# Low parts of the queries stored between zeros, so that products over 64 rows become products over 128, with an 8 KB descriptor scratch

## The chip, the cores and the metric

The kernel runs on one core of a Trainium2 chip. The time is device microseconds of one execution of the whole program, from inputs in HBM to the output in HBM; the figure for the kernel before is the median of three runs. TensorE (PE) does the matrix products, and its weight loads (PEld) are profiled beside them. VectorE (DVE), ScalarE (ACT) and GpSimd (POOL) do the elementwise work, SyncE (SP) issues most of the DMAs, POOL the others.

## The reference, cut to what matters

A trunk of four pre-norm residual layers over 512 tokens of width 1024. Layers 0 and 3 use differential attention (8 heads, two softmax maps each), layer 1 stick-breaking attention (16 heads), layer 2 sliding-window attention (16 query heads, 4 key heads). In all of them a query and a key have 64 channels, so that a score is a product over 64 channels:

```python
s = jnp.einsum('bqhjd,bkhjd->bhjqk', qb, k).astype(jnp.float32) * scale + bias   # layers 0, 3
z = jnp.einsum('bqhd,bkhd->bhqk', qb, k).astype(jnp.float32) * scale              # layer 1
s = jnp.einsum('bnqgrd,bnkgd->bngrqk', q, kb).astype(jnp.float32) * (SW_DIM ** -0.5) + bias  # layer 2
```

Each layer ends with a gated feed-forward block: an up projection to twice 2752 channels, a causal convolution of width 3, SiLU gate times value, and a down projection from 2752 channels, which are 21 blocks of 128 and a rest of 64.

## The kernel before

The residual lies with channels on the partitions, in eight chunks of 128 x 512. A product of float32 operands is made of three products of their high and low parts (`mm3`): high times high, high times low, low times high, summed in one bank of PSUM. The weights come in pieces of four 128 x 128 blocks through four raw tiles; ACT makes the high part, DVE the low part, each into a ring of four tiles. SP issues the weight loads in the order of use.

All work is written as tasks, and a planner emits each instruction in the order of its estimate of the engines' clocks. The result is one fixed queue per engine; an engine that waits holds up what stands behind it. The planner charges a product of n columns n / 2.4 ns (107 at least), whatever its number of rows, and 600 ns for a DMA on SP. It knows nothing of memsets, which are emitted when a layer's tiles are made.

**Queries and keys.** `to_qk` takes a projected chunk of 128 channels, which holds two heads or maps of 64 channels (its halves). DVE scales it out of PSUM into `qk_t`, ACT copies it to `hi`, POOL subtracts to make the low part, and four DMAs on SP stack the parts for each half: a query's high part twice (`qs`, 128 rows), a key's high and low part (`ks`, 128 rows). One product over 128 rows then gives two of the three terms. The third, a query's low part times a key's high part, is a product over the 64 rows of that half, read directly from the tile in which POOL put the low part (`ql`, ring of two, given back when the query's scores are done). The low parts of keys have a ring of one.

**Scores.** In layers 0, 2 and 3 `scores` makes both halves in four products: two over 128 rows (L665), then the two over 64 rows, one in the upper and one in the lower rows (L668). Layer 1 has the keys as weights, and alternates one product over 128 rows (L943) with one over 64 (L944).

**Down projection.** Each output chunk is 63 products over 128 rows and a tail for the last 64 channels: `gt_hl` has their high part in the upper and their low part in the lower 64 rows, `wt_hi` the weights' high part twice (L1341, 128 rows), `wt_lo` the weights' low part once (L1342, 64 rows). The last chunk of the last layer is made in two halves of 256 tokens.

Of the kernel before, what the change touches and what calls it, by code (L numbers as in the profile page):

```python
# [12 lines left out]
F32R = mybir.dt.float32r  # L13
# [22 lines left out]
# blocks of 128 rows per weight piece: inputs of width D, and of the down projection  # L36
KD = (4, 4)
KF = (4, 4, 4, 3, 3, 3)
# the very first pieces, for the first row block and for the others
FIRST = [(0, 1), (1, 4)], [(0, 4)]  # L40
# order of the output projection's (output chunk, head chunk) blocks: what needs the last heads comes late
# [23 lines left out]
# The work is written as tasks, generators that yield what they need next: an engine for an operation of some  # L65
# nanoseconds, which they emit when resumed; a tile of a ring; an event; or a delay. Everything is emitted in the
# order of an estimate of the engines' clocks, so that no engine's queue stands still for what another has yet to do.
# [33 lines left out]
class Ring:  # L101
    """Tiles in turn. Some users leave a few spare for those that must not starve."""
# [44 lines left out]
class Clock:  # L147
# [58 lines left out]
    def run(self, tasks):  # L206
        """Emit until these tasks are through."""
        while True:
            while self.todo:
                task, value = self.todo.popleft()  # L210
                self.t = task.t
                self.resume(task, value)
            if all(t.end.at is not None for t in tasks):
                return
            self.pick()
# [3 lines left out]
def trunk(ctx: ExitStack, tc: tile.TileContext, A, out):  # L219
# [60 lines left out]
    # the last product of all comes in halves of the tokens  # L280
# [48 lines left out]
    def rstd(ms, r, scale, cols=slice(0, T)):  # L329
        """r <- 1 / sqrt(scale * ms + EPS), the approximate root refined by a Newton step; ms is a bank, given back."""  # L330
        n = cols.stop - cols.start
        ms_, r = ms[:, :n], r[:, cols]
        lt = yield tmps
        ln = lt[:, :n]
        yield act(n, -2)
        nc.scalar.activation(ln, ms_, AF.Ln, scale=scale, bias=eps)
        vt = yield tmps
        v = vt[:, :n]
        yield dve(n, prio=-2)
        nc.vector.tensor_scalar(v, ms_, scale, EPS, ALU.mult, ALU.add)  # L340
        banks.give(ms)
        yield act(n, -2)
        nc.scalar.activation(r, ln, AF.Exp, scale=-0.5)
        tmps.give(lt)
        yield dve(n, 3, -2)
        nc.vector.scalar_tensor_tensor(v, v, -0.5, r, ALU.mult, ALU.mult)
        nc.vector.tensor_tensor(v, v, r, ALU.mult)
        nc.vector.scalar_tensor_tensor(r, v, 1.5, r, ALU.add, ALU.mult)
        tmps.give(vt)

    class Norm:
        """Takes the residual chunk by chunk; the gain goes in at once, the reciprocal root is applied later."""
# [68 lines left out]
    class LastNorm(Norm):  # L421
        """The last chunk comes in halves of the tokens, so that the first half's way out is hidden."""
# [79 lines left out]
    def product(pieces, parts, last=True, cols=slice(0, T)):  # L502
        """One product; returns its bank."""
        t = cols.stop - cols.start
        ps = yield banks
        k, K = 0, sum(pieces)
        for n in pieces:
            w = yield w_next()
            wh, wl = w_view(w)
            for j in range(n):  # L510
                xh, xl = yield parts[k]
                yield mm(t, t, t, prio=5)
                mm3(ps[:, :t], wh[:, j, :], wl[:, j, :], xh[:, cols], xl[:, cols], k == 0, last and k == K - 1)
                k += 1
            w_done(w)
        return ps

    def split_psum(ps, hi, lo, n=T):
        """A bank into two rings' tiles; gives the bank back."""
        h = yield hi  # L520
        yield act(n)
        copy(h[:, :n], ps[:, :n], AF.Copy)
        l = yield lo
        yield dve(n)
        nc.vector.tensor_tensor(l[:, :n], ps[:, :n], f(h[:, :n]), ALU.subtract)
        banks.give(ps)
        return h, l

    class Forms:
        """What an attention's projections become."""  # L530

        def __init__(self, pool, norm, l, v_bufs=3):
            self.norm, self.l = norm, l
            self.qk_t = ring(pool, "qk_t", 1)
            self.hi = ring(pool, "hi", 1, dtype=F32R)
            self.lo = {"q": ring(pool, "ql", 2, dtype=F32R), "k": ring(pool, "kl", 1, dtype=F32R)}
            self.st = {n: ring(pool, n + "s", 2, (P, 2, T), F32R) for n in "qk"}
            self.vh = ring(pool, "vh", v_bufs, dtype=F32R)
            self.vl = ring(pool, "vl", v_bufs, dtype=F32R)

        def values(self, got):
            """Two units' values, tokens on the partitions."""
# [20 lines left out]
        def to_v(self, ps, got):  # L563
            """Split [tokens of a block, (block, channels)] per unit."""
# [22 lines left out]
        def to_qk(self, ps, got, name, flip=False, lo_dve=False):  # L587
            """Split, and stacked for the products of 64 rows to take two terms at once. Per half of the channels:
            a query's high part twice, a key's high and low part. flip reverses the tokens within each block, as
            the bands of the biases want them."""  # L590
# [14 lines left out]
            lo = yield self.lo[name]  # L605
# [6 lines left out]
            for dst, src in ((st[top, 0], hi[top]), (st[bot, 1], hi[bot]), (st[bot, 0], other[top]), (st[top, 1], other[bot])):  # L612
                yield dma(-1)
                nc.sync.dma_start(out=f(dst), in_=f(src))
            clock.t += DMA_LAT
            self.hi.give(hi)
            if name == "k":
                self.lo[name].give(lo)
            got.set((st, lo))

        def q_done(self, q):
            self.st["q"].give(q[0])
            self.lo["q"].give(q[1])
# [4 lines left out]
        def first(self, us, flip):  # L628
            """The first two units' queries and keys, row block by row block as the residual arrives."""
# [17 lines left out]
        def qkv(self, us, flip):  # L647
            """All units' projections."""
# [12 lines left out]
    def scores(dst, q, k, qs, ks):  # L661
        """Both halves' products; those of 64 rows side by side, in the array's two halves."""
        (q2, ql), (k2, _) = q, k
        for half in range(2):
            nc.tensor.matmul(dst[half], q2[:, half, qs], k2[:, half, ks], start=True, stop=False)  # L665
        for half in range(2):
            rows = slice(64 * half, 64 * half + 64)
            nc.tensor.matmul(dst[half], ql[rows, qs], k2[rows, half, ks], start=False, stop=True)  # L668

# [73 lines left out]
    # per key block: which of three tiles its weights are in, and from which column  # L743
# [151 lines left out]
    def stick_attention(pool, norm, l, oh, ol, done, last_bank):  # L895
# [35 lines left out]
        def logit_steps():  # L931
            for i, hd in enumerate(heads):
# [3 lines left out]
                rows = slice(64 * half, 64 * half + 64)  # L936
                for kb in reversed(range(NB)):
# [6 lines left out]
                    nc.tensor.matmul(zb[:, :n], k2[rows, half, ks], ql[rows, kb * P:], start=False, stop=True)  # L944
# [24 lines left out]
        def weight_steps():  # L969
            for hd in heads:  # L970
                b = yield banks.spare(1)
                last = None
                for kb in reversed(range(NB)):
# [5 lines left out]
                    if last:  # L979
                        # the later block's sums, from those behind a key to those over the whole block  # L980
# [44 lines left out]
    def window_attention(pool, norm, l, oh, ol, done, last_bank):  # L1025
# [113 lines left out]
        def turn_steps(ats):  # L1139
            """Each half's weights turned, key blocks 0 and 1 into one tile, 2 and 3 into another."""  # L1140
# [14 lines left out]
        def value_steps(ats):  # L1155
            """Both halves at once, of which a half of the rows counts each. The banks have two query blocks each."""
# [65 lines left out]
    def feed_forward(pool, l, norm, nxt):  # L1222
# [8 lines left out]
        # the last 64 rows of the down projection, twice, to take both parts of g at once  # L1231
        wt_hi = pool.tile([P, D], F32R, name="wt_hi")
        wt_lo = pool.tile([P, D], F32R, name="wt_lo")
        g = [event() for _ in range(NFF)]
# [70 lines left out]
        def steps():  # L1305
            e = None
            # the first two side by side, while the last of the residual is on its way
# [24 lines left out]
            for m in range(ND):  # L1332
                ms = slice(m * P, m * P + P)
                halves = l == DEPTH - 1 and m == ND - 1
                for cols in (slice(0, T // 2), slice(T // 2, T)) if halves else (slice(0, T),):
# [6 lines left out]
                    nc.tensor.matmul(ps[:, :n], wt_lo[0:64, ms], gt_hl[0:64, cols], start=False, stop=True)  # L1342
# [49 lines left out]
def kmajor(w):  # L1392
    """[K, M] -> [M/128, 128 of K, K/128, 128 of M]"""
# [4 lines left out]
def layout(inp):  # L1398
    """Data layout only."""
# [5 lines left out]
    for l, w in enumerate(wq):  # L1405
        # queries and keys in chunks of 128 channels, values in groups of 256
# [8 lines left out]
    # the first two heads' queries and keys, all four chunks for a block of rows at a time  # L1415
# [20 lines left out]
    # constants of the shapes  # L1436
# [30 lines left out]
```

## Time and profile before

| | |
|---|---|
| median of three runs | 2419.07 us (2418.07 to 2422.58) |
| profiled execution: span from first to last instruction | 2418.2 us |
| PE / PEld busy | 2387.7 / 1939.6 us |
| DVE / ACT / POOL busy | 1620.8 / 1227.9 / 375.5 us |
| matrix products | 11271 |
| HBM read, mean rate over the span | 212.15 MB, 89 GB/s |

The span is that of the one execution that was profiled; its own time outside the profiler's span is not recorded, and the median of the three unprofiled runs lies 0.9 us above the span. A product's duration in the profile includes the time in the pipeline, so durations of neighbours overlap; distances between starts tell how fast PE takes them. In a row of PE, 64*128 means 64 rows of the array by 128 columns of weights, and 64x512 that 512 columns are moved through it.

### The profile page before, as it was taken

To read this page: it belongs to the slowest core of one execution; us is meant where nothing else is said; L and a number is where in the kernel's file an instruction comes from. 1 tells how busy PE (TensorE), PEld (TensorE's weight loads), DVE (VectorE), ACT (ScalarE), POOL (GpSimd) and SP (SyncE) were. 2 spreads that over 40 slices of the span, in tenths; PEclk is the share of its full clock that TensorE was granted. 3 is DMA by queue.
4 is the path that set the end of the run, shared out by engine and by line. 5 is a ranking of instruction groups with operands and counts; after the bars stand their busy time and mean duration, and the time that the engine had idled before them with its cause. 6 is when DMAs were issued, how large, how long until landed. Compare 5 with 4: busy or idle time off the path is not lost.

```text
span 2418.2 us, 32917 instructions
## 1 busy us (share of the span) xinstructions
PE 2387.7 (99%) x11271; PEld 1939.6 (80%) x11271; DVE 1620.8 (67%) x3054; ACT 1227.9 (51%) x2413; POOL 375.5 (16%) x385
## 2 busy tenths in 40 slices
PE   8999999999999999999999999999999999999998
PEld 6888788877877787888778888888778887888876
DVE  6886877733598878777335858776336876877624
ACT  4675544433476656444335855454334665544433
POOL 3442200000143322000001320000012433000001
PEclk9999999999999999999999999999999999999999
DMA  6442323233322223333334423333334442333333
GB/s 191 142 135 88 96 97 108 94 89 92 115 79 79 83 63 98 97 105 94 89 93 133 109 74 105 97 105 92 90 110 129 138 127 70 105 100 105 93 88 104
DMA packets 139031, 247.93 MB, mean 103 GB/s; under 512 B 17487, under 2 KB 32495, under 8 KB 138864
## 3 DMA queue, kind: packets, MB, share of 16 engines
q1 hardware_dynamic: 134736, 233.18, 31.7%
q0 software_dynamic: 4128, 12.66, 1.9%
q8 instruction: 88, 1.44, 0.2%
q14 instruction: 79, 0.65, 0.1%
HBM read 212.15 MB, written 2.16 MB: 89 GB/s over the span
## 4 chain that ended last, share of the span: by engine, by line
PE 62%; DVE 3%; ACT 1%; issue 1%; DMA 1%; POOL 0%; SPq 0%; DVEq 0%; ACTq 0%; POOLq 0%
PE ps L498 19%; PE ps L499 18%; PE ps L500 18%; PE ps L556 2%; PE ps L668 1%; DVE h_lo L366 1%; PE ps L665 1%; PE ps L1151 1%; DVE w_lo L291 1%; PE ps L1342 0%; PE ps L870 0%; PE ps L944 0%; DVE x L1197 0%; DMA ks<-kl 0%; PE ps L1341 0%
## 5 line engine op out<-in xcount | busy, mean ns | idle before, releaser
L288 ACT ACTIVATE w_hi<-w_raw 128x512 fp32r<-128x512 f32 (+2 forms) x775 | 477.5, 617 | 844.5 <-PE ps L499 691.8
L291 DVE TENSOR_TENSOR w_lo<-w_raw,w_hi 128x512 fp32r<-128x512 f32 (+2 forms) x775 | 535.0, 692 | 431.0 <-ACT w_hi L288 423.6
L498 PE MATMUL ps<-h_hi,w_hi 128*128 128x512 f32 x1840 | 728.6, 396 | 5.6 <-ACT h_hi L364 5.6
L499 PE MATMUL ps<-h_lo,w_hi 128*128 128x512 f32 x1840 | 721.5, 392 | 0.7
L500 PE MATMUL ps<-h_hi,w_lo 128*128 128x512 f32 x1840 | 719.4, 391 | 2.5 <-DVE w_lo L291 2.5
L498 PEld LDWEIGHTS ps<-h_hi,w_hi 128*128 128x128 f32 x1840 | 346.9, 189 | 84.6 <-ACT h_hi L364 5.6
L499 PEld LDWEIGHTS ps<-h_lo,w_hi 128*128 128x128 f32 x1840 | 347.1, 189 | 77.1 <-DVE h_lo L366 9.3
L500 PEld LDWEIGHTS ps<-h_hi,w_lo 128*128 128x128 f32 x1840 | 346.9, 189 | 75.6 <-DVE w_lo L291 2.9
L498 PE MATMUL ps<-gh,w_hi 128*128 128x512 f32 (+1 forms) x693 | 272.4, 393 | 0.0
L499 PE MATMUL ps<-gl,w_hi 128*128 128x512 f32 (+1 forms) x693 | 269.2, 388 | 0.0
L500 PE MATMUL ps<-gh,w_lo 128*128 128x512 f32 (+1 forms) x693 | 269.1, 388 | 0.0
L1242 DVE TENSOR_TENSOR ut<-ps,r_bc 128x512 f32<-128x512 f32 x172 | 118.5, 691 | 176.8 <-PE ps L500 176.8
L381 POOL TENSOR_TENSOR acc<-tmp,tmp 128x512 f32<-128x512 f32 x9 | 11.7, 1300 | 1041.3 <-ACT tmp L373 1041.3
L1247 ACT ACTIVATE y<-ut,c_conv 128x512 f32<-128x512 f32 x172 | 140.2, 815 | 44.0 <-DVE ut L1242 44.0
L498 PEld LDWEIGHTS ps<-gh,w_hi 128*128 128x128 f32 x693 | 130.2, 188 | 35.2 <-ACT w_hi L288 6.7
L500 PEld LDWEIGHTS ps<-gh,w_lo 128*128 128x128 f32 x693 | 130.3, 188 | 29.6
L499 PEld LDWEIGHTS ps<-gl,w_hi 128*128 128x128 f32 x693 | 130.2, 188 | 28.4
L1249 DVE SCALAR_TENSOR_TENSOR y<-ut,c_conv,y 128x512 f32<-128x512 f32 x172 | 128.5, 747 | 21.6 <-ACT y L1247 21.4
L1250 DVE SCALAR_TENSOR_TENSOR y<-ut,c_conv,y 128x512 f32<-128x512 f32 x172 | 129.3, 752 | 6.1
L381 POOL TENSOR_TENSOR acc<-acc,tmp 128x512 f32<-128x512 f32 x53 | 77.2, 1456 | 309.8 <-ACT tmp L373 293.5
L556 PE MATMUL ps<-w_hi,h_hi 128*128 128x256 f32 x416 | 120.6, 290 | 0.0
L556 PE MATMUL ps<-w_lo,h_hi 128*128 128x256 f32 x416 | 117.5, 282 | 0.0
(203 smaller groups left out, 3389.2 us busy)
## 6 DMA issues: line engine op xcount, KB each, us to landing
w_raw<-in_w_up_dram SPq DMA_DIRECT2D x344, 256.0 KB, 2.6
w_raw<-in_w_qk_dram SPq DMA_DIRECT2D x108, 256.0 KB, 2.8
w_raw<-in_w_down_dram SPq DMA_DIRECT2D x99, 256.0 KB, 2.6
w_raw<-in_w_down_dram SPq DMA_DIRECT2D x99, 192.0 KB, 2.3
qs<-hi SPq DMA_DIRECT2D x128, 128.0 KB, 3.0
w_raw<-in_w_o_dram SPq DMA_DIRECT2D x64, 256.0 KB, 2.7
w_raw<-in_w_v_dram SPq DMA_DIRECT2D x52, 256.0 KB, 2.7
bias<-rows_da POOLq DMA_DIRECT2D x16, 512.0 KB, 4.7
```

Of the source, the lines that this page charges most:

```text
L288: copy(hi[:, :n], raw[:, :n], AF.Copy)
L291: nc.vector.tensor_tensor(lo[:, :n], raw[:, :n], f(hi[:, :n]), ALU.subtract)
L366: nc.vector.scalar_tensor_tensor(h_lo[d], x[d], g, f(h_hi[d]), ALU.mult, ALU.subtract)
L381: nc.gpsimd.tensor_tensor(acc, self.first if n == 2 else acc, sq, ALU.add)
L498: nc.tensor.matmul(ps, wh, xh, start=start, stop=False, **kw)
L499: nc.tensor.matmul(ps, wh, xl, start=False, stop=False, **kw)
L500: nc.tensor.matmul(ps, wl, xh, start=False, stop=stop, **kw)
L556: nc.tensor.matmul(dst, a[:, ts], c[:, j, :], start=k + b + n == 0, stop=k == ND - 1 and n == 2, skip_group_check=True)
L1242: nc.vector.tensor_tensor(u[:, 2:T + 2], ps, r, ALU.mult)
L1247: nc.scalar.activation(y, u[:, 2:T + 2], AF.Identity, scale=cw[:, 2:3], bias=cw[:, 3:4])
L1249: nc.vector.scalar_tensor_tensor(y, u[:, 1:T + 1], cw[:, 1:2], y, ALU.mult, ALU.add)
L1250: nc.vector.scalar_tensor_tensor(y, u[:, 0:T], cw[:, 0:1], y, ALU.mult, ALU.add)
```

## The change

The low part of a query gets a layout with one plane per half, in which the other half's 64 rows are zero. The zeros are written once per layer by POOL, and two DMAs per query chunk put the low part's halves into their places. The third term of a score then is a product over 128 rows: the zeros meet the key's low part. `scores` makes the two terms of a half one behind the other. The ring of low parts before stacking is one tile for queries and keys together, and is given back when the transfers have been issued. In the down projection the lower 64 rows of `wt_lo` are set to zero, and the tail's second product runs over 128 rows. The scratch for DMA descriptors is set to 8192 bytes. The diff also takes out comments and docstrings, which are left out here.

```diff
@@ class Forms
-            self.lo = {"q": ring(pool, "ql", 2, dtype=F32R), "k": ring(pool, "kl", 1, dtype=F32R)}
+            self.lo = ring(pool, "lo", 1, dtype=F32R)
             self.st = {n: ring(pool, n + "s", 2, (P, 2, T), F32R) for n in "qk"}
+            self.ql = ring(pool, "ql", 2, (P, 2, T), F32R)
+            for _, _, t in self.ql.free:
+                nc.gpsimd.memset(f(t)[64:P, 0], 0.0)
+                nc.gpsimd.memset(f(t)[0:64, 1], 0.0)
...
@@ to_qk
-            lo = yield self.lo[name]
+            lo = yield self.lo
...
-            for dst, src in ((st[top, 0], hi[top]), (st[bot, 1], hi[bot]), (st[bot, 0], other[top]), (st[top, 1], other[bot])):
+            moves = [(st[top, 0], hi[top]), (st[bot, 1], hi[bot]), (st[bot, 0], other[top]), (st[top, 1], other[bot])]
+            ql = None
+            if name == "q":
+                ql = yield self.ql
+                moves += [(ql[top, 0], lo[top]), (ql[bot, 1], lo[bot])]
+            for dst, src in moves:
                 yield dma(-1)
                 nc.sync.dma_start(out=f(dst), in_=f(src))
             clock.t += DMA_LAT
             self.hi.give(hi)
-            if name == "k":
-                self.lo[name].give(lo)
-            got.set((st, lo))
+            self.lo.give(lo)
+            got.set((st, ql))
 
         def q_done(self, q):
             self.st["q"].give(q[0])
-            self.lo["q"].give(q[1])
+            self.ql.give(q[1])
...
@@ scores
-        (q2, ql), (k2, _) = q, k
+        k2 = k[0]
         for half in range(2):
-            nc.tensor.matmul(dst[half], q2[:, half, qs], k2[:, half, ks], start=True, stop=False)
-        for half in range(2):
-            rows = slice(64 * half, 64 * half + 64)
-            nc.tensor.matmul(dst[half], ql[rows, qs], k2[rows, half, ks], start=False, stop=True)
+            for n, part in enumerate(q):
+                nc.tensor.matmul(dst[half], part[:, half, qs], k2[:, half, ks], start=n == 0, stop=n == 1)
...
@@ logit_steps
-                rows = slice(64 * half, 64 * half + 64)
...
-                    nc.tensor.matmul(zb[:, :n], k2[rows, half, ks], ql[rows, kb * P:], start=False, stop=True)
+                    nc.tensor.matmul(zb[:, :n], k2[:, half, ks], ql[:, half, kb * P:], start=False, stop=True)
...
@@ feed_forward
+        nc.gpsimd.memset(f(wt_lo)[64:P], 0.0)
...
-                    nc.tensor.matmul(ps[:, :n], wt_lo[0:64, ms], gt_hl[0:64, cols], start=False, stop=True)
+                    nc.tensor.matmul(ps[:, :n], wt_lo[:, ms], gt_hl[:, cols], start=False, stop=True)
...
@@ kernel
-    nc = _bacc.Bacc("TRN2", target_bir_lowering=False, num_devices=1)
+    nc = _bacc.Bacc("TRN2", target_bir_lowering=False, num_devices=1, dynamic_dma_scratch_size=8192)
```

## Rows read from the trace of the kernel before

**Rows 1.** The page's busy time, share of the span and instructions of each engine.
```profile
PE 2387.7 (99%) x11271; PEld 1939.6 (80%) x11271; DVE 1620.8 (67%) x3054; ACT 1227.9 (51%) x2413; POOL 375.5 (16%) x385
```

**Rows 2.** Timeline of PE in a down projection: start us, duration us, line, tiles, form.
```profile
502.33 0.39 PE L500 MATMUL ps<-gh,w_lo 128*128 128x512 f32 x1
502.56 0.39 PE L1341 MATMUL ps<-gt_hl,wt_hi 128*128 128x512 f32 x1
502.88 0.49 PE L1342 MATMUL ps<-gt_hl,wt_lo 64*128 64x512 f32 x1
503.31 0.50 PE L498 MATMUL ps<-gh,w_hi 128*128 128x512 f32 x1
503.64 0.40 PE L499 MATMUL ps<-gl,w_hi 128*128 128x512 f32 x1
```

**Rows 3.** Source view of the 64-row products: count, ns min/median/max, first and last start, forms.
```profile
L668 PE MATMUL ps<-ks,ql x192: 322/381/581, 56.7 to 2001.3; 64*128 64x256 f32 x80, 64*128 64x128 f32 x48, 64*128 64x384 f32 x32, 64*128 64x512 f32 x32
...
L944 PE MATMUL ps<-ql,ks x64: 322/436/792, 645.2 to 869.0; 64*128 64x128 f32 x16, 64*128 64x256 f32 x16, 64*128 64x384 f32 x16, 64*128 64x512 f32 x16
...
L1342 PE MATMUL ps<-gt_hl,wt_lo x33: 382/492/492, 502.9 to 2406.7; 64*128 64x512 f32 x31, 64*128 64x256 f32 x2
```

**Rows 4.** Timeline of PE in layer 0, scores of 256 columns.
```profile
57.75 0.40 PE L665 MATMUL ps<-ks,qs 128*128 128x256 f32 x2
58.08 0.39 PE L668 MATMUL ps<-ks,ql 64*128 64x256 f32 x2
...
58.73 0.39 PE L499 MATMUL ps<-h_lo,w_hi 128*128 128x512 f32 x1
```

**Rows 5.** Timeline of PE in layer 3, scores of 512 columns.
```profile
2000.60 0.73 PE L665 MATMUL ps<-ks,qs 128*128 128x512 f32 x2
...
2002.03 0.39 PE L499 MATMUL ps<-ol,w_hi 128*128 128x512 f32 x1
```

**Rows 6.** Timeline of PE in layer 1: first and ninth of nine products in a row.
```profile
756.60 0.22 PE L943 MATMUL ps<-qs,ks 128*128 128x128 f32 x1
...
759.22 0.33 PE L943 MATMUL ps<-qs,ks 128*128 128x128 f32 x1
```

**Rows 7.** Timeline of PE in layer 1, two neighbours of 256 columns.
```profile
772.06 0.28 PE L556 MATMUL ps<-w_hi,h_hi 128*128 128x256 f32 x1
772.17 0.28 PE L556 MATMUL ps<-w_lo,h_hi 128*128 128x256 f32 x1
```

**Rows 8.** Windows of layer 1: us; busy PE, PEld, DVE, ACT, POOL; clock; DMA share; GB/s.
```profile
640.00:890.00 250.00, 243.37 (x1260) 195.40 (x1260) 214.31 (x490) 167.42 (x411) 88.53 (x81) 0.98 0.27 80
650.00:700.00 50.00, 49.52 (x247) 38.96 (x247) 44.89 (x110) 38.65 (x98) 23.36 (x22) 1.00 0.32 93
700.00:750.00 50.00, 48.31 (x258) 38.74 (x257) 47.73 (x112) 37.06 (x91) 18.65 (x17) 1.00 0.21 64
750.00:800.00 50.00, 48.50 (x246) 38.93 (x246) 38.02 (x84) 32.03 (x80) 14.45 (x14) 0.90 0.26 77
800.00:850.00 50.00, 47.08 (x250) 37.91 (x248) 44.86 (x98) 30.97 (x75) 19.05 (x16) 1.00 0.31 90
```

**Rows 9.** PE's waits in layer 1: us in total, times, longest us.
```profile
PE ps L499 <- DVE al L965: 3.2, 4, 1.1
```

**Rows 10.** Groups of POOL's instructions: count, busy us, mean ns, idle before.
```profile
L607 POOL TENSOR_TENSOR ql<-qk_t,hi 128x512 fp32r<-128x512 f32 x24 | 33.0, 1375 | 78.0 <-ACT hi L604 73.8 <-PE ps L944 3.2 <-PE ps L500 1.0
...
L789 POOL TENSOR_SCALAR ns<-ns,rl 128x512 f32<-128x512 f32 x16 | 17.1, 1068 | 23.6 <-DVE rl L785 17.5 <-ACT r_o L343 3.2 <-ACT tmp L336 1.4
...
L1229 POOL MEMSET ut<- 128x2 f32 x12 | 0.7, 100 | 0.0
```

**Rows 11.** Timeline of POOL between layers 0 and 1, with the idle time before.
```profile
616.33 1.28 POOL L381 TENSOR_TENSOR acc<-acc,tmp 128x512 f32<-128x512 f32 x1 [15.03 <-ACT tmp L373]
```

**Rows 12.** DMA issues of the stacked queries: count, KB each, median us to landing.
```profile
qs<-hi SPq DMA_DIRECT2D x128, 128.0 KB, 3.0
```

**Rows 13.** Waits of SP's queue for a free raw tile of weights: us, times, longest us.
```profile
SPq L299 <- DVE w_lo L291: 1663.1, 700, 10.4
```

## The prediction

> **What bounds the kernel now.** I read the page's busy shares first, then the order of the matrix products in time around each edited line, then windows by stage, the waits, and the rows of POOL and the DMAs. The shares [rows 1] name TensorE: PE is busy for 2387.7 of 2418.2 us, DVE for 67%. A pipelined PE shows busy even when it does little, so the reader has to look at the distance from one start to the next. In the down projection [rows 2] two products over the whole array that move 512 columns start 0.23 us apart (502.33 to 502.56). Behind the last of them the product of 64 rows comes after 0.32 us instead of 0.23, the next full one after 0.43, the one behind that after 0.33. From 502.56 to 503.64 there are three starts in 1.08 us where the cadence would give 0.69: 0.39 us is lost in which no engine is waited for. That is the quantity the change works on, and everything else in the sum is about whether it can be kept.
>
> **How often.** The 64-row products [rows 3]: 33 in the down projection (one each), 192 in the scores of layers 0, 2 and 3 (96 pairs: 24 with 128 columns, 40 with 256, 16 each with 384 and 512), 64 in the stick-breaking layer (16 of each width). The change gives each of them all 128 rows. Products and weight loads stay the same in number; only their form changes.
>
> **Down projection.** 33 x 0.39 = 12.9 us. Nothing else limits this stage (PE follows its cadence on both sides), so I take all of it.
>
> **Pairs.** Here the old form has a merit. The two 64-row products of a pair are merged in the timeline and take hardly more time than one, and this is lost. At 256 columns [rows 4], from 57.75 to 58.73 four products of 256 and one of 512 take 0.98 us. Products of 256 over the whole array start 0.11 us apart, 0.12 with rounding [rows 7], so the new form would need 4 x 0.12 + 0.23 = 0.71: 0.27 won. At 512 columns [rows 5], from 2000.60 to 2002.03 is 1.43 against 5 x 0.23 = 1.15, or 0.28; but the second product there started late behind the previous pair (as the third start in [rows 2] does, by 0.10), which I count with that pair, so 0.18. For 384 columns I take the middle, 0.22, for 128 the 0.27 of 256. Sum: 64 x 0.27 + 16 x 0.22 + 16 x 0.18 = 23.7 us.
>
> **Single ones of the stick-breaking layer.** Between 756.60 and 759.22 [rows 6] four full and four 64-row products of 128, 256, 384 and 512 columns alternate: 2.62 us. Full cadence would be 2 x (0.12 + 0.12 + 0.175 + 0.23) = 1.29, with 384 columns put between its neighbours. That is 1.33 for four; with the fourth's late successor (0.10), 0.36 each. 64 x 0.36 = 23.0 us. All three terms: 59.6 us.
>
> The Trainium skill (TensorEngine Tiling (Array Packing), Key Properties) says that changing the tiling mode, though not the tile, drains the engine. The trace agrees as far as it can: extra time stands before and behind each group of 64 rows, 0.39 us around a single one [rows 2], and none inside a pair.
>
> **What DVE takes back.** In the stick-breaking stage DVE is busy for 214.31 of 250 us [rows 8], and by 50 us: 44.89, 47.73, 38.02, 44.86. About 5.1 us of the savings fall in each of these four stretches. PE already stands still for DVE there, 3.2 us on one line alone [rows 9]. If no stretch can get DVE above 97%, 700 to 750 shrinks by 0.8 us only, its neighbours by 3.7 and 3.8, 750 to 800 by the full 5.1: 13.4 of 20.5, so 7 us are given back. Bounds: 0, because PE can do projection products in DVE's time, and 15, if the three full stretches don't shrink at all. I take 7, nearer to the windows.
>
> **What is added.** (1) 64 DMAs, two per query chunk, of 128 KB. Their like land in 3.0 us [rows 12]. The low part used to be read where POOL wrote it; now it arrives some 3 us later, behind POOL's subtraction. What is late next is a score of that head, but in three layers the matching key is projected after the query and goes the same way, and in the sliding-window layer, where the keys come first, a score waits those 3 us at most. On SP's queue the weight pieces stand behind the two DMAs, which wait for POOL; that queue has waited 1663 us in total for a free raw tile [rows 13], so it runs ahead by far and the hold costs nothing while pieces are ready. Without that cover, in the first heads of four layers, I bound it by 0 and 3 us a layer, and take 2 in all. (2) One low tile for queries and keys instead of three: the next low part waits until the last transfers from it have landed, some 1.4 [rows 10] + 3 us after its high part, while the chunk behind it needs a product of 24 x 0.23 = 5.5 us first. Nothing, up to 1 us a layer. (3) Memsets on POOL, which has no row of that size: above a memset of 128x2 at 0.10 us, below a scaling of 128x512 at 1.07 [rows 10]. Four half tiles per attention layer stand in POOL's queue before the last addition to the norm's sums, where POOL idles for 15.03 us [rows 11]. They may have to wait for the tiles of the feed-forward layer that lie in their place, and if that lasts to its last product at 612, four at 1.07 end at 616.3, as the addition starts: nothing, up to 2 us at three layers. The feed-forward memset has the same cover. I take 1 us for all. (4) Smaller descriptor scratch: no row shows POOL waiting for descriptors; nothing, a few us if one issue had to wait for a landing. (5) The planner's costs for the products are unchanged, but two DMAs more per query move later tasks by 1.2 us in its estimate, so single products change places: 3 us either way, zero taken.
>
> **Sum.** 59.6 - 7 - 2 - 1 = 49.6, against the profiled span: 2418.2 - 49.6 = 2368.6. The median of the runs shown is 0.9 above that span. I say 2369.
>
> **Rivals.** *DVE becomes the bound of all attention stages.* The stick-breaking stage keeps 8 of 23, the pairs half of 23.7, the down projection its 12.9; less 4 for delays, 29 are won: 2389. For it speaks that in 700 to 750 DVE is already at 95%; against it that PE's named waits are few [rows 9] and PE is busy for 243.37 of 250 us.
>
> *Nothing is given back and the clock stays up.* Between 750 and 800 the granted clock averages 0.90 [rows 8], right behind the dense stretch of 64-row products in [rows 6]: 10 us at 1.2 instead of 2.4 GHz, which cost 5. If the fall goes away with the changes of form, and DVE keeps up, it is 2418.2 - 59.6 - 5 = 2354. Against it: waits for DVE get longer, and they could bring the fall too.
>
> *The other side: the intervals don't come from the form, and the overlap of the pairs is lost.* Then only the pairs change: 24 x 0.11 + 40 x 0.12 + 16 x 0.175 + 16 x 0.23 = 13.9 us more, 2433. It decides if a full product in that place still starts late. Against it: the full product on the same operand just ahead starts after 0.23 [rows 2].
> The Trainium skill has the rule for this (same page, When to Use Tiling: a contraction of 64 rows or fewer suits two row tiles, ideally twice as fast); the trace shows that gain inside a pair and a larger loss around it.
>
> *The late low part stalls PE, which works in order.* To eat 50 us, each of 32 queries would have to stop PE for 1.6 us; weight pieces wait split in four tiles of 12 products (2.8 us) each, so SP would have to be held for over 10 us. Time about 2420.
>
> **Chances.** Forecast 0.70 (own range 2358 to 2380), DVE bound 0.14, everything kept 0.10, late low part 0.03 (no change), overlap lost 0.03. The range takes in the second and third up to their values: 2354 to 2390. A measurement tells 0.2% (4.8 us) from no change. Faster 0.94, same 0.03, slower 0.03.
>
> **What would show it.** No matrix form with 64 rows but the same number of products; the three starts behind the down projection's tail product 0.23 us apart; that stage 3 us shorter in each layer, the up projection unchanged; the stick-breaking stage some 16 us shorter with DVE above 90% and longer PE waits for DVE; two new transfers per query; memsets well under 1.07 us inside POOL's idle time. I am wrong if starts stay late in the full form, if PE waits for query transfers or the norm's sums by more than a few us, or if DVE's waits eat over half of the stick-breaking term.

## The result, and the profile after

The kernel after takes 2388.3 us (median of 4 runs, 2388.1 to 2389.0) against 2420.0 for the kernel before (2418.1 to 2422.6): ratio 0.987, 95% interval 0.9858 to 0.9882, 31.7 us less. 2369 was forecast, with 2354 to 2390 as the range. The way is right, and about three fifths of the forecast gain of 51 us came.

The page of the kernel after, its span and its first line:

```profile
span 2386.3 us, 33050 instructions
...
PE 2337.6 (98%) x11271; PEld 1943.6 (81%) x11271; DVE 1620.2 (68%) x3054; ACT 1225.1 (51%) x2413; POOL 382.1 (16%) x405
```

Against [rows 1], the same 11271 products keep PE busy for 50.1 us less, but PE idles for 48.7 us instead of 30.5. So 18.2 us of what was won stand there again as waits. The timeline of PE in a down projection, which answers to [rows 2]:

```profile
503.73 0.39 PE L500 MATMUL ps<-gh,w_lo 128*128 128x512 f32 x1
503.96 0.39 PE L1348 MATMUL ps<-gt_hl,wt_hi 128*128 128x512 f32 x1
504.19 0.39 PE L1349 MATMUL ps<-gt_hl,wt_lo 128*128 128x512 f32 x1
504.43 0.39 PE L498 MATMUL ps<-gh,w_hi 128*128 128x512 f32 x1
504.66 0.39 PE L499 MATMUL ps<-gl,w_hi 128*128 128x512 f32 x1
```

From 503.96 to 504.66 are the three starts that took 1.08 us; they take 0.70. In a pair of scores of layer 0, the answer to [rows 4], the second half's two products of 256 columns stand 0.12 us apart, and the next follows at 0.11:

```profile
60.78 0.28 PE L675 MATMUL ps<-ks,qs 128*128 128x256 f32 x1
60.90 0.28 PE L675 MATMUL ps<-ks,ql 128*128 128x256 f32 x1
61.01 0.39 PE L498 MATMUL ps<-h_hi,w_hi 128*128 128x512 f32 x1
```

The source view has no form with 64 rows left, in the same numbers as [rows 3] (L675 is now both kinds of score product):

```profile
L675 PE MATMUL ps<-ks,ql x192: 272/282/397, 60.2 to 1972.6; 128*128 128x256 f32 x80, 128*128 128x128 f32 x48, 128*128 128x384 f32 x32, 128*128 128x512 f32 x32
...
L950 PE MATMUL ps<-ql,ks x64: 273/308/397, 645.6 to 849.4; 128*128 128x128 f32 x16, 128*128 128x256 f32 x16, 128*128 128x384 f32 x16, 128*128 128x512 f32 x16
...
L1349 PE MATMUL ps<-gt_hl,wt_lo x33: 279/394/394, 504.2 to 2375.0; 128*128 128x512 f32 x31, 128*128 128x256 f32 x2
```

PE's waits by what ended them (us in total, times, longest us). Those for DVE's `al` and `z` were 3.2 [rows 9] and 3.0 us in the kernel before, the one for a key's stacked parts 1.4:

```profile
PE ps L499 <- DVE al L971: 6.1, 9, 1.9
PE ps L988 <- DVE z L960: 5.4, 9, 1.3
PE ps L498 <- ACT h_hi L364: 5.4, 1, 5.4
PE ps L675 <- DMA ks<-lo: 4.7, 7, 1.2
PE ps L877 <- DVE a L799: 3.8, 6, 0.9
...
PE ps L498 <- ACT at0h L1122: 2.3, 2, 1.2
PE ps L1157 <- DVE nm L1068: 1.3, 2, 0.8
```

The waits for `at0h` and `nm` lie in the sliding-window layer, where the trace of before names no wait of PE at all. By stage, in us: an attention stage runs from the last start of a product that reads `gl` in the layer before (in layer 0 from the first product) to the last that reads `oh`; all are worked out from the starts of PE's products in each trace.

```
run                                attention 0      1      2      3 | down (layers 0 to 2; 3)
before                             245.6   304.3  167.8  242.3 | 122.8; 124.7
after                              247.2   285.5  171.0  236.1 | 120.1; 121.3
E1  down projection only           246.1   299.7  167.4  240.3 | 120.1; 121.3
E2  new form, old order            242.4   285.3  162.7  234.8 | 120.1; 121.3
E3  old form, new order            248.0   300.8  176.5  244.4 | 122.8; 124.7
E4  scratch only                   247.1   300.2  167.8  242.3 | 122.8; 124.7
E5  one of two DMAs charged        245.1   285.7  169.2  238.9 | 120.1; 121.3
E6  three DMAs charged             243.9   281.5  165.7  238.8 | 120.1; 121.3
E7  20 splits on POOL              244.0   290.0  162.9  233.6 | 120.1; 121.3
E8  al twice                       242.9   324.1  162.7  235.4 | 120.1; 121.3
E9  40 low weight parts left out   243.5   270.9  162.5  232.8 | 120.1; 121.3
E10 own low tiles                  243.4   285.7  162.7  235.8 | 120.1; 121.3
E11 old order in layer 2 only      245.0   286.6  162.5  235.7 | 120.1; 121.3
E12 three charged in layer 1 only  244.4   281.6  163.0  235.5 | 120.1; 121.3
```

The up projections (236.8 to 237.0 everywhere) are left out. The 304.3 of before holds the 10 us at 1.2 GHz of [rows 8]; E4, whose queues are the same, had the full clock in that stage and 300.2. The table shows where the gain is missing: layer 0, for which the terms gave 8 x (0.27 + 0.27 + 0.22 + 0.18) = 7.5 us, and layer 2, with 32 x 0.27 = 8.6, have become longer. In layer 0 the clock has a part in this. The windows of the first 60 us (columns as in [rows 8]), of the kernel after and of the kernel before:

```profile
0.00:60.00 60.00, 50.53 (x243) 40.70 (x244) 35.98 (x60) 27.73 (x52) 22.86 (x32) 0.94 0.59 189
```
```profile
0.00:60.00 60.00, 51.30 (x252) 41.11 (x253) 37.97 (x70) 29.39 (x57) 22.11 (x29) 1.00 0.62 192
```

With a second fall of 3.4 us at 186 us, the kernel after spends 10.2 us of this stage at 1.2 GHz, which cost 5.1 if PE was busy throughout (an estimate); the kernel before spends none of it there, E2 and E4 3.4 us each.

### The profile page after: what moved, and what is told of

Read it like the earlier page. It is cut to its first block, busy times and chain, and to the rows that moved or that the text cites. A ratio compares the mean times of both kernels' runs of the same rounds, so it can differ in the third digit from the quotient of the medians.

```text
span 2386.3 us, 33050 instructions
## 1 busy us (share of the span) xinstructions
PE 2337.6 (98%) x11271; PEld 1943.6 (81%) x11271; DVE 1620.2 (68%) x3054; ACT 1225.1 (51%) x2413; POOL 382.1 (16%) x405
## 4 chain that ended last, share of the span: by engine, by line
PE 59%; DVE 5%; ACT 1%; DMA 1%; issue 1%; POOL 0%; SPq 0%; DVEq 0%; ACTq 0%; POOLq 0%
PE ps L499 18%; PE ps L500 18%; PE ps L498 18%; PE ps L561 2%; PE ps L675 1%; DVE w_lo L291 1%; DMA ks<-lo 1%; DVE h_lo L366 1%; DVE a L799 0%; ACT ns L783 0%; PE ps L1157 0%; DVE ns L779 0%; DVE vl L581 0%; PE ps L992 0%; DVE x L1203 0%
```

## The experiments

**E1: the down projection alone.**

```diff
 (kernel before)
+        nc.gpsimd.memset(f(wt_lo)[64:P], 0.0)
...
-                    nc.tensor.matmul(ps[:, :n], wt_lo[0:64, ms], gt_hl[0:64, cols], start=False, stop=True)
+                    nc.tensor.matmul(ps[:, :n], wt_lo[:, ms], gt_hl[:, cols], start=False, stop=True)
```

> Kernel before, with only the down projection's tail product over 128 rows. If the intervals around a 64-row product come from its form, each of the 33 tails gives back 0.39 us: 12.9 us less, 2407 against 2420. If the overlap rule holds and the intervals come from something else, no change: 2420.

Measured: 2406.3 against 2420.0, ratio 0.9938 (0.9919 to 0.9956). The intervals come from the form. A down stage as cut in the table (first to last product that reads `gl`) holds 7 of its 8 tails: 7 x 0.39 = 2.7 us, as measured; the last tail falls to the attention stage behind it.

**E2 and E3: form and order apart.** The added DMAs change the planner's estimate and so the order in which everything is handed out. E2 has the new form without that, E3 that without the new form. In E2 the queues of DVE and ACT are instruction for instruction those of before, in E3 those of after but for one memset of 33 x 16, and PE's differ only within a score.

```diff
 (E2: kernel after)
+            ql = (yield self.ql) if name == "q" else None
             lo = yield self.lo
...
-            for dst, src in moves:
-                yield dma(-1)
+            for i, (dst, src) in enumerate(moves):
+                if i < 4:
+                    yield dma(-1)
                 nc.sync.dma_start(out=f(dst), in_=f(src))
 (E3: kernel before, after the loop over a query's or key's four transfers)
+            if name == "q":
+                yield dma(-1)
+                yield dma(-1)
```

> Kernel after, but the planner isn't charged for the two added DMAs of a query and hands out the query's low tile where it handed it out before; VectorE's and ScalarE's queues are then instruction for instruction those of the kernel before. Theory A, that most of what was won and lost again (59.6 promised, 31.7 came) went into the changed order of the work: 2370, 18 us below the kernel after, with the sliding-window layer some 8 us shorter than in the kernel before instead of longer. Theory B, that VectorE takes the savings back whatever the order: 2388, as the kernel after.

> Kernel before, but the planner is charged for two more DMAs per query, which are not issued; VectorE's and ScalarE's queues are then those of the kernel after. Theory A: the order alone costs 10 to 18 us, 2430 to 2438. Theory B: order is worth nothing, 2420.

Measured: E2 2372.3, ratio 0.9796 (0.9779 to 0.9813); E3 2429.7, ratio 1.0038 (1.0025 to 1.0051). The order alone costs 9.7 us with the old form and 2388.3 - 2372.3 = 16 us with the new one; E3 came out just under the bound I gave. Half of it lies in the sliding-window stage: 171.0 against 162.7, and 176.5 against 167.8. With the new form 4.8 us more lie in layer 0 (247.2 against 242.4), and 3.4 of these are the clock by the count above. That part need not come from the order: the first fall lasts 6.8 us in E8 as in the kernel after, and E8 has E2's order in that layer. The windows of the sliding-window stage's late part (us; busy PE, PEld, DVE, ACT, POOL; granted clock; DMA share; GB/s), first of the kernel after:

```profile
1292.00:1340.00 48.00, 47.99 (x276) 41.68 (x275) 37.98 (x123) 39.16 (x118) 16.76 (x27) 1.00 0.59 152
1340.00:1372.00 32.00, 25.94 (x156) 21.33 (x155) 26.20 (x93) 26.80 (x86) 11.44 (x20) 0.95 0.46 119
```

and of E2, shifted by its earlier start of the stage:

```profile
1288.00:1336.00 48.00, 46.93 (x280) 40.36 (x278) 40.08 (x129) 41.78 (x131) 18.70 (x30) 1.00 0.61 153
1336.00:1368.00 32.00, 31.70 (x194) 27.44 (x194) 27.73 (x90) 26.29 (x79) 11.12 (x17) 1.00 0.39 110
```

In the kernel after, the last projection product starts 89.1 us into the stage, in E2 105.6. These products use the norm's output and weight parts, for which PE does not wait anywhere in this stage, and fill PE's time between scores, turns and values. Used up early, they are missing in the last 30 us of the attention, as I read the two pairs of windows: PE stands still for 6 us there, some 3 us run at 1.2 GHz (a granted clock of 0.95 over 32 us), and 156 products are done where E2 does 194.

**E4: the descriptor scratch alone.**

```diff
-    nc = _bacc.Bacc("TRN2", target_bir_lowering=False, num_devices=1)
+    nc = _bacc.Bacc("TRN2", target_bir_lowering=False, num_devices=1, dynamic_dma_scratch_size=8192)
```

> Kernel before with the descriptor scratch of 8 KB alone. If the smaller scratch holds POOL's DMAs up, a few us more than 2420; if nothing ever fills it, 2420 within the measurement.

Measured: ratio 1.0002 (0.9991 to 1.0014). No cost shows.

**E5 and E6: how much the planner is charged** (E2 with other numbers in place of 4: `i < 5`, so one of a query's two added DMAs is charged, and `i < 3`, for queries and keys).

> As the new form in the old order (2372), but the planner is charged for one of a query's two added DMAs. If what the order costs grows with the time by which the planner thinks a query's stacked parts late, this lies between 2372 and 2388: about 2380, and in the sliding-window layer the projections end between the two. If the old order is only a lucky one, the time need not lie between.

> As the new form in the old order, but the planner is charged for three DMAs of every query and key instead of four: scores are handed out still earlier against the projections. If the cost grows with the lateness in the plan, 2365 to 2372. If the planner's old figure was about right, scores come before their transfers have landed, PE waits for them, and it is slower: 2374 to 2385, with PE's waits for query and key transfers above 10 us.

Measured: E5 2388.4, ratio 0.9868 (0.9851 to 0.9886); E6 2378.5, ratio 0.9837 (0.9819 to 0.9855). The first theory falls: half the charge costs as much as all of it. In E6 PE's waits for a key's parts grow to 7.2 us, short of the 10 that I named, and still it is slower than E2. What does hold, in the sliding-window stage, is the link with the projections. By their last start, in us into the stage, and the stage's length: 89.1 and 171.0 (after), 93.2 and 169.2 (E5), 96.8 and 165.7 (E6), 105.6 and 162.7 (E2). With the old form it is the same: 93.7 and 176.5 (E3) against 109.7 and 167.8 (before). That the early end is the reason, and not something else that moves with the same order, was not shown: no run moved the projections alone.

**E7, E8 and E9: DVE's load in the stick-breaking stage.** All three change E2 and leave the plan as it is; in E9 the products read what an earlier piece left in the tile, so that it shows the time alone.

```diff
 (E7: in w_split; on_pool holds the first and last stream numbers of layer 1's projections)
-        nc.vector.tensor_tensor(lo[:, :n], raw[:, :n], f(hi[:, :n]), ALU.subtract)
+        engine = nc.gpsimd if on_pool[0] + 8 <= i < on_pool[1] and i % 2 else nc.vector
+        engine.tensor_tensor(lo[:, :n], raw[:, :n], f(hi[:, :n]), ALU.subtract)
 (E8: in weights)
             nc.vector.tensor_tensor(al, z, f(ah), ALU.subtract)
+            nc.vector.tensor_tensor(al, z, f(ah), ALU.subtract)
 (E9: in w_split)
+        if not on_pool[0] + 8 <= i < on_pool[1]:
             nc.vector.tensor_tensor(lo[:, :n], raw[:, :n], f(hi[:, :n]), ALU.subtract)
```

> As the new form in the old order, but 20 of the weight pieces of the stick-breaking layer are subtracted on POOL instead of VectorE, with the plan unchanged: 13.8 us of VectorE's work leave the stage, 29 go to POOL. Theory, that VectorE's load in this stage took 8 of the 23 us: the stage, 285 us from the last tail product to the last block of the output projection, loses 4 to 8 us, PE's waits for VectorE there shrink, 2365 to 2368. Rival, that the waits come from the length of the chain through the attention's own operations: 285 stays.

> As the new form in the old order, but VectorE makes the low part of the stick-breaking weights twice (64 operations, 38 us more of its work in that stage, same result). If VectorE is the limit there, most of the 38 us appear in the stage: 25 to 38, 2397 to 2410. If PE is, less than 15 appear, since VectorE has idle time.

> As the new form in the old order (2372), but the low parts of 40 weight pieces of the stick-breaking layer are left out (the products read what an earlier piece left in the tile): 27.7 us of VectorE's work go, nothing is put anywhere else, the attention's own chain is untouched. Theory, that VectorE's load took 8 of the 23 us: the stage falls from 285 to 277 to 280, 2364 to 2367. Rival, that the chain's length makes the waits: 285 and 2372 stay.

Measured: E7 2377.8, ratio 0.9831 (0.9816 to 0.9847); E8 2412.9, ratio 0.9968 (0.9957 to 0.998); E9 2358.7, ratio 0.9748 (0.9734 to 0.9763). The stage went from 285.3 to 290.0, 324.1 and 270.9. The same window in E2 and in E9, and PE's waits for DVE in E9's stage, which were 5.2 and 5.5 us in E2:

```profile
640.00:870.00 230.00, 217.48 (x1229) 186.96 (x1228) 211.60 (x488) 164.49 (x409) 88.91 (x82) 1.00 0.32 92
```
```profile
640.00:870.00 230.00, 226.64 (x1294) 198.89 (x1293) 195.63 (x462) 168.20 (x415) 85.84 (x82) 1.00 0.35 98
...
PE ps L994 <- DVE z L966: 1.8, 4, 0.7
PE ps L505 <- DVE al L977: 1.4, 3, 0.5
```

With 40 subtractions gone (DVE's work on `w_lo` is 503.6 us in all instead of 533.5) and the attention's own operations untouched, PE's waits shrink from 10.7 to 3.2 us and the stage by 14.4, more than the 8 that I had put down to DVE. That DVE's load takes back part of the gain here is shown by this. E8 says the same from the other side: 64 operations added, which make DVE's work on `al` 81.6 us instead of 37.3, lengthen the stage by 38.8 us. Not all of that is direct, as its window and waits show: a clock of 0.96 over 250 us stands for 20 us at 1.2 GHz, which cost 10, behind more standstills of PE.

```profile
640.00:890.00 250.00, 214.46 (x1155) 180.43 (x1153) 239.86 (x530) 161.37 (x401) 82.06 (x77) 0.96 0.29 81
...
PE ps L499 <- DVE al L972: 23.5, 27, 1.6
PE ps L989 <- DVE z L960: 12.3, 9, 2.1
```

E7 missed both expectations: work left DVE and the stage grew. DVE's other operations became slower beside the busier POOL, and PE's waits for DVE in the stage grew from E2's 10.7 us to 15.5, while those for POOL stayed at 1.0 us or less:

```profile
PE ps L505 <- DVE al L977: 8.2, 13, 1.4
PE ps L994 <- DVE z L966: 7.3, 9, 2.1
```

Groups of DVE in the window of 640 to 870 (count, busy us, mean ns, idle before), E2 and then E7:

```profile
L928 DVE SCALAR_TENSOR_TENSOR u<-z,u 128x512 f32<-128x512 f32 x16 | 12.9, 805 | 0.0
...
L928 DVE SCALAR_TENSOR_TENSOR u<-z,u 128x128 f32<-128x128 f32 x16 | 7.2, 451 | 0.6 <-issue 0.6
```
```profile
L934 DVE SCALAR_TENSOR_TENSOR u<-z,u 128x512 f32<-128x512 f32 x16 | 14.5, 908 | 0.0
...
L934 DVE SCALAR_TENSOR_TENSOR u<-z,u 128x128 f32<-128x128 f32 x16 | 9.1, 569 | 0.6 <-issue 0.6
```

**E10: own low tiles for queries and for keys** (E2).

```diff
-            self.lo = ring(pool, "lo", 1, dtype=F32R)
+            self.lo = {n: ring(pool, f"lo_{n}", 1, dtype=F32R) for n in "qk"}
...
-            lo = yield self.lo
+            lo = yield self.lo[name]
...
-            self.lo.give(lo)
+            self.lo[name].give(lo)
```

> As the new form in the old order, but queries and keys have a low tile of their own instead of one together. If the shared tile costs time (POOL stands 20 us for landings out of it), 2366 to 2370 and POOL's waits for these landings go. If POOL's waiting is covered, 2372 within the measurement.

Measured: 2376.1, ratio 0.9817 (0.9802 to 0.9831), which overlaps E2's interval. POOL's standstill for the landing of transfers out of the shared tile (12.4 and 8.2 us in E2, 17.5 in the kernel after for keys alone) is gone, and no stage is shorter. It was covered.

**E11 and E12: the order layer by layer** (the kernel after with `ql` taken as in E2, and the charge by layer).

```diff
 (E11)
+                if i < (4 if self.l == 2 else 6):
+                    yield dma(-1)
 (E12)
+                if i < (3 if self.l == 1 else 4):
+                    yield dma(-1)
```

> Kernel after, but the two added DMAs aren't charged in the sliding-window layer, so that this layer alone has the old order. Theory, that half of what the new order costs lies in this layer: its stage 162 to 164 instead of 171, 2380. If the order of the layers hangs together, the stage stays near 171 and 2388.

> As the new form in the old order, but three DMAs charged per query and key in the stick-breaking layer, whose stage was 281.5 with that plan against 285.3, and four in the others. If the stages add up, 2368. If the 281.5 was chance, 2372.

Measured: E11 2378.0, ratio 0.9829 (0.9812 to 0.9845); E12 2369.3, ratio 0.9793 (0.9778 to 0.9807). The order of the sliding-window layer alone is worth 10.3 us, and its stage is back at 162.5. E12's stick-breaking stage is 281.6, as in E6, but against E2 the 3 us lie within both intervals. E2 and E12 beat both kernels: 2.0 and 2.1% below before, against 1.3% for the kernel after.

## Why the prediction was right, and what in it was not

**The intervals belong to the form: right.** PE's starts are at full cadence wherever 64 rows stood before, and E1 alone wins 13.7 us (10.6 to 19.6 by its interval) where 12.9 were worked out. The rival that only the overlap of the pairs would be lost is out. The rule on draining in the Trainium skill (TensorEngine Tiling (Array Packing), Key Properties) holds here: with no change of form left, the 0.39 us around each tail product is gone.

**DVE takes 7 of 23 us in the stick-breaking stage: right.** With the same plan and the full clock it went from 300.2 (E4) to 285.3 (E2): 14.9 won, of which 0.4 is the last tail of the layer before, so 14.5 of 23.0; 8.5 were given back. The 23.0 themselves hold: compared product by product, the distances between starts around the changed products, where PE does not wait, are 22.8 us shorter in E2 than in E4, and all those with a wait of PE are together 7.6 us longer (worked out from the starts in both traces). E9 shows that DVE's load is what holds the stage. The mechanism is the one forecast too, with DVE full in the stretch around 700 to 750, as its window in E2 shows (a little above the 97% that I had set as the limit):

```profile
690.00:740.00 50.00, 45.71 (x260) 38.91 (x259) 49.65 (x115) 36.57 (x91) 20.24 (x17) 1.00 0.23 70
```

**Pairs, 23.7 us: too much.** With the plan unchanged (E2 against before and E4), and 0.4 for the tail taken off, layer 3 gives 7.1 of 7.5, layer 2 4.7 of 8.6 and layer 0 3.2 to 4.7 of 7.5: 15 to 16.5 in all. Pair by pair, where neither E4 nor E2 has a wait, 256, 384 and 512 columns win 0.28, 0.23 and 0.17 to 0.27 us, about as worked out. For 128 columns I had taken the 0.27 of 256 without a row; they win 0.18, which is 2 us less over the 24 pairs. Such a pair and the next start in the kernel before, then in E2:

```profile
1836.51 0.34 PE L665 MATMUL ps<-ks,qs 128*128 128x128 f32 x2
1836.78 0.33 PE L668 MATMUL ps<-ks,ql 64*128 64x128 f32 x2
1837.04 0.50 PE L665 MATMUL ps<-ks,qs 128*128 128x256 f32 x2
```
```profile
1800.91 0.22 PE L675 MATMUL ps<-ks,qs 128*128 128x128 f32 x1
...
1801.30 0.33 PE L675 MATMUL ps<-ks,qs 128*128 128x256 f32 x1
```

Here 0.53 us become 0.39, and the start behind was another 0.04 late before. The rest of what is missing stands as waits in layers 0 and 2, for which I had set aside 2 us in all. In layer 2 it is mainly one wait of E2 for an added transfer:

```profile
PE ps L675 <- DMA ql<-lo: 1.0, 1, 1.0
```

In layer 0 PE waits for DVE's `a`, `at0l` and `nm`, 2.1 us in E2 against 0.5 in E4; what makes these waits was not tried.

**The planner, "3 us either way, zero taken": the step that failed.** The order that the added charge brought cost 16 us, nearly all of the distance between 2369 and 2388: without it, E2's 2372 lies 3 us from the forecast. That E2 comes so close is in part luck, as the pairs gave less than forecast and the clock more: leaving out the last 7 us, the traces of before and of after have 13.7 us at 1.2 GHz each and that of E2 6.8, worth 3.4 us at full work (an estimate). Whether this share of the 16 us follows from the order is open. I had looked at how far single products move, and not at what a different order of a whole layer does: in the sliding-window layer it alone cost 10.3 us (E11), most likely because nothing is left to fill PE when the projections run ahead of the scores. The shift was also larger than my 1.2 us, since the planner adds 0.2 us behind each charged operation of a task: 2 x 0.8.

**The rivals.** The time is that of "DVE becomes the bound of all attention stages" (2389), but not for its reason: with DVE's queue back in the old order the loss in layer 2 is gone (E2, E11). So it is luck that 2388 lies in the range: its upper end had been set to take in this rival, and the forecast's own range ended at 2380. "Everything kept, clock up" did not happen. The clock fell in other places than in [rows 8], behind standstills of PE in layers 0 and 2, and its mean is 0.996 as before. How long PE stood still does not decide it alone: on the two lines where it waits longest in the first 30 us, E1 has 5.2 and 2.8 us and keeps the full clock, E10 5.1 and 2.8 (and 0.2 on a third) and a fall of 3.4 us. The late low part hardly stalled PE: the kernel after has no named wait for `ql`, E2 the one of 1.0 us, and the shared tile was covered (E10).

**Memsets, transfers, scratch: right.** The memsets took 0.52 us each in the attention layers and 0.95 in the feed-forward (POOL's groups: count, busy us, mean ns):

```profile
L541 POOL MEMSET ql<- 64x512 f32 x8 | 4.2, 522 | 20.3 <-issue 10.6 <-PE ps L1348 9.4
L542 POOL MEMSET ql<- 64x512 f32 x8 | 4.2, 520 | 0.4
L1240 POOL MEMSET wt_lo<- 64x1024 f32 x4 | 3.8, 948 | 6.9 <-PE ps L499 6.8
```

Between layers 0 and 1 two of them wait for the last tail product, and are done 3 us before the addition of [rows 11] comes:

```profile
610.54 0.52 POOL L541 MEMSET ql<- 64x512 f32 x1 [9.41 <-PE ps L1348]
611.11 0.52 POOL L542 MEMSET ql<- 64x512 f32 x1
614.61 1.29 POOL L381 TENSOR_TENSOR acc<-acc,tmp 128x512 f32<-128x512 f32 x1 [2.97 <-ACT tmp L373]
```

The new transfers land in the time of their like [rows 12]:

```profile
ql<-lo SPq DMA_DIRECT2D x64, 128.0 KB, 3.0
```

Open: why layer 3 is at 238.8 to 238.9 in E5 and E6 but at 234.8 in E2 (a second fall of the clock there, of 3.4 us, explains 1.7 of E6's 4 us; E5 and E2 have one each), and why the stick-breaking stage doesn't depend on the charge except when it is three.

## What to carry to other kernels

Look at the distances between starts around every product whose array form differs from its neighbours': here each single change there and back cost about 0.4 us (0.3 at 128 columns), and padding with zeros to the common form was the cheaper way even where two half-height products had run side by side. Where a planner hands out the work, a change of its costs is a change of the kernel: measure the new form under the old order and the old form under the new order before saying what either is worth. Look, too, at where the filler ends, the work for which an engine never waits: in the sliding-window stage here the time grew the earlier the projections ended.

## What the runs showed of the hardware that I had not expected

POOL's work slows DVE's: with 20 subtractions moved from DVE to POOL (E7), an operation of DVE that reads two tiles took 908 ns instead of 805 at 512 columns and 569 instead of 451 at 128, and DVE's busy time in the window rose from 211.60 to 213.44 us with 17 instructions fewer. The Trainium skill (SBUF — State Buffer, SBUF: two separate sides) says that the two engines share a pair of ports, which one instruction takes for itself. The trace agrees in that DVE's operations became longer beside the added POOL work; that the port is the reason no run here isolates.

More standstills went with a lower clock in the stick-breaking stage: with 35.8 us of named waits of PE for DVE (E8) 20 us of it ran at 1.2 GHz, with 10.7 (E2) and 15.5 (E7) none.
